# Moving loads to where their places come free in a one-core hybrid decoder step

## The chip, the cores and the metric

One core of a Trainium2 chip runs the whole program. TensorE (PE) does the matmuls, VectorE (DVE) and ScalarE (ACT) empty its PSUM banks and do the elementwise work, GpSimd (POOL) does little but issue stores, SyncE (SP) issues nearly all loads. The metric is the time of one execution in microseconds (us) on the device; lower is better. A profiled execution also has a span, from its first to its last instruction.

## The reference

One layer over 1024 prompt tokens and 8 sample tokens, all float32, width 1024. One input projection feeds three branches; each is gated, projected, and the sum goes through an output projection.

```python
h = rmsnorm(x, norm_gain)
proj = h @ w_in                                   # (T, 1024) x (1024, 10256)
q, k, v, gla_g, a_lr, u, pool_g, xq, xg, merge = split(proj)
o, S = gla_chunked(q, k, v, log_sigmoid(a_lr @ w_a2 + b_a) / 16, S0)   # 4 heads, 128 x 256 states
br_gla  = rmsnorm(o) * silu(gla_g)
br_pool = multiscale_pool(u, hist) * silu(pool_g)          # windows 2, 4, 8, 16
br_x    = cross_attn(xq, mem_k, mem_v) * silu(xg)          # 4 heads, 256 memory rows
merged  = sum_n sigmoid(merge_n) * (br_n @ w_branch[n])
y = rmsnorm(x + merged @ w_out)
```

For the prompt, the memory keys and values come from `mem_prompt`; for each of the 8 samples they are read from caches, as are the linear-attention state and the pooling history. New states, histories and memories are outputs too.

## The kernel before

Every large product is done in a split form: each float32 operand becomes a high and a low part (`split`: ScalarE writes the high part, VectorE the rest), and `mm3` does three matmuls, high by high, high by low, low by high.

The input projection runs in 36 pairs of 256 columns (`Pair`). Each pair is a 2 x 2 block product done with seven block products (Strassen's form); one product is 24 matmuls of 258 columns, in two halves `c`. `seq` is the order of all 252 products, `prepare` splits the left operands AHEAD products before they are used. A pair's weights arrive in two raw tiles (`raw`, three buffers); the first holds a11 and a21, the second a12 and a22. The sums of operands use `ws` tiles, the split parts `w2` tiles, two per product.

The mixers (cross attention, then linear attention, then pooling) are generators of steps. They are written between the products: after each half product, `fill` runs a `Stream` until the costs it has been given reach a target that grows with the slot number. Stream A holds cross and linear attention, stream B pooling. `mem` makes memory keys and values before that.

The order of instructions on TensorE and SyncE is the order in which they are written. For the other engines a planner orders them by its own estimates. Each queue is worked off in order: an instruction that waits holds all behind it.

Places for tiles: `R` is a shared ring of NR tiles of 128 x 512 (loads, split parts, outputs of the mixers), `V` four tiles of that size (sample loads kc, qb, vc, s0, vb, and raw output weights), `E` thirty tiles of 128 x 1032, `W2` ten, `PZ` two PSUM banks for the mixers, `PX` six for the products. A load into a tile waits on SyncE until the place is free.

For the samples of a head, cross attention writes their queries to memory (`xq_scr`) and reads them back spread over all partitions (`qb`), beside the cached keys (`kc`); `vc` are cached values. Linear attention does the same with `v_scr`, `vb` and the states `s0`. Both read-backs are issued from GpSimd's queue, the others from SyncE's. A stored branch output goes to `mix_scr` (`mixsc`) and is read back when its gate is ready.

After the pairs, 24 units of 72 matmuls do the branch projections (`fetch` loads and splits weights, one unit ahead), and then nine blocks of tokens are multiplied by `w_out`, whose 16 pieces `w_out_unit` loads and splits: `hf` is the half of the columns, `k` the row block.

Of the kernel before, what the change touches and what calls it, by code (L numbers as in the profile page):

```python
# [35 lines left out]
NE = 30  # L36
NR = 11
WORK_A, WORK_B = 500.0, 100.0
WINDOWS = (2, 4, 8, 16)
# [8 lines left out]
def trunk_kernel(ctx: ExitStack, tc: tile.TileContext,  # L48
# [75 lines left out]
    def W2(name, dt=F32R):  # L124
        return wk.tile([P, 4, P], dt, tag="w2", name=name, bufs=10)

# [98 lines left out]
    def split_r(src, shape, name, scale=None):  # L225
        hi, lo = R(shape, F32R, name + "h"), R(shape, F32R, name + "l")
        split(hi, lo, src, scale)
        return hi, lo

    def mm3(out, lh, ll, rh, rl, start, stop, more=False):  # L230

        nc.tensor.matmul(out, lhsT=lh, rhs=rh, start=start, stop=False, skip_group_check=more)  # L232
        nc.tensor.matmul(out, lhsT=lh, rhs=rl, start=False, stop=False, skip_group_check=more)  # L233
        nc.tensor.matmul(out, lhsT=ll, rhs=rh, start=False, stop=stop, skip_group_check=more)  # L234
# [37 lines left out]
    class Pair:  # L272


        def __init__(self, src, dst, s0=None, gated=None):
            self.src, self.dst, self.s0, self.gated = src, dst, s0, gated

        def load(self):
            self.raw = []
            for i in range(2):  # L280
                raw = RAW("raw")
                nc.sync.dma_start(out=raw, in_=self.src.rearrange("(k p) n -> p k n", p=P)[:, 4 * i:4 * i + 4])
                self.raw.append(raw)

        def operands(self):
            lo, hi = self.raw
            a11, a12, a21, a22 = lo[:, :, :P], hi[:, :, :P], lo[:, :, P:], hi[:, :, P:]

            def of(x, y, op):
                s = wk.tile([P, 4, P], F32, tag="ws", name="ws", bufs=3)  # L290
                nc.vector.tensor_tensor(s, x, y, op=op)
# [12 lines left out]
            yield parts(s1, "s1")  # L304
            yield parts(of(a11, a21, ALU.subtract), "s3")
            yield parts(of(a12, s2, ALU.subtract), "s4")
            yield parts(a22, "a22")
# [21 lines left out]
    RIGHT = ("11", "21", "t2", "t1", "t3", "22", "t4")  # L329
    AHEAD = 4  # L330
    left, prep = {}, {"n": 0}

    def prepare(n):

        while prep["n"] < min(n + 1, len(seq)):
            i, j = seq[prep["n"]]
            p = pairs[i]
            if j == 0:
                p.gen = p.operands()
            left[i, j] = next(p.gen)  # L340
            if j == 2 and i + 1 < NPAIR:
                pairs[i + 1].load()
            prep["n"] += 1

    pairs[0].load()
    for tb in range(4, 8):
# [235 lines left out]
    def cross_memory(h):  # L582
        mk, mv = cross["raw", h]
        t = PZ()
        for i in range(2):
            for a in range(2):
                nc.tensor.transpose(t[:, i * NM + a * P:i * NM + (a + 1) * P], mk[:, a, i * P:(i + 1) * P], ident)
        cross["mk", h] = split_r(t.rearrange("p (i m) -> p i m", i=2), [2, NM], "mkT")
        cross["mv", h] = split_r(mv, [2, DV], "mvs")
# [43 lines left out]

    def cross_sample(h):

# [7 lines left out]
        nc.gpsimd.dma_start(out=xq_scr[h], in_=qn[:NS])  # L643
        yield 1.2
        sc = wk.tile([P, 16], F32, tag="sc", name="sc", bufs=2)
        for b2 in range(4):
            qb = V([2, DV], name="qb")
            nc.gpsimd.dma_start(out=qb, in_=xq_scr[h][2 * b2:2 * b2 + 2].partition_broadcast(P))
            for bb in range(2):
                b = 2 * b2 + bb  # L650
                kc = loaded(ck[b, :, h, :].rearrange("(a p) d -> p a d", p=P), [2, DV], "kc", V)
                for a in range(2):
                    nc.vector.tensor_tensor_reduce(kc[:, a, :], kc[:, a, :], qb[:, bb, :],
                                                   scale=1.0, scalar=0.0, op0=ALU.mult, op1=ALU.add,
                                                   accum_out=sc[:, a * NS + b:a * NS + b + 1])
            yield 2.2
        yield 0.5
        yield 0.5
        yield 0.5
# [43 lines left out]
    def cross_steps():  # L703
# [14 lines left out]
        cross_load(0)  # L718
        cross_memory(0)
        yield 2  # L720
        cross_queries(0, 0)
        for s in range(16 + 2):
# [5 lines left out]
            if s % 4 == 3 and s < 15:  # L728
                cross_load(s // 4 + 1)
            if s >= 1:  # L730
                yield next(samples, 0)
            if 0 <= s - 2:
                values(s - 2)
                yield 1.7
            if s % 4 == 3 and s < 15:
# [125 lines left out]

    def gla_sample(h):

# [5 lines left out]
        nc.gpsimd.dma_start(out=v_scr[h], in_=vs[:NS])  # L869
        yield 1  # L870
        t = PZ()
# [8 lines left out]

        def states(b0):
            s0 = loaded(st_gla[b0:b0 + 2, h].rearrange("b k v -> k b v"), [2, DV], "s0", V)
            vb = V([2, DV], name="vb")
            nc.gpsimd.dma_start(out=vb, in_=v_scr[h][b0:b0 + 2].partition_broadcast(P))
            for i in range(2):
# [7 lines left out]
        sq = wk.tile([P, 2], F32, tag="sqs", name="sqs", bufs=2)  # L893
        for i in range(2):
            s0 = []
# [9 lines left out]
            nc.scalar.activation(t[:, :DV], t[:, :DV], AF.Square, accum_out=sq[:, i:i + 1])  # L905
            yield 1
        r = rstd_of(sq, 1.0 / DV)
        for i in range(2):
# [12 lines left out]
    def gla_steps():  # L921
# [7 lines left out]
        for n in range(N + 1):  # L929
# [8 lines left out]
            if n > 0:  # L938
                gla_recur(ph, 2 * pc + 1)
                yield 2  # L940
            if n < N:
                gla_within(h, 2 * c + 1)
                yield 2
                if n + 2 < N:
# [8 lines left out]
            if n >= 2:  # L953
                for _ in range(2):
                    yield next(samples, 0)
# [4 lines left out]

    def pool_steps():
        for g, w in enumerate(WINDOWS):
            raw = loaded(pool_w[g].rearrange("(k p) n -> p k n", p=P), [2, DV], "pwr")
            pw = split_r(raw, [2, DV], "pw")
            hist = R([DV], name="hist")
            nc.sync.dma_start(out=hist[:NS * HIST], in_=st_pool.rearrange("b j c -> (b j) c")[:, g * DV:(g + 1) * DV])
            us = smp_of(S_U + 2 * g, 2)
# [98 lines left out]
    class Stream:  # L1066


        def __init__(self, steps, work, first, last):
            self.steps, self.work, self.first, self.last, self.done = steps, work, first, last, 0  # L1070

        def run(self, slot):
            while self.done < self.work * (slot - self.first) / (self.last - self.first):
                cost = next(self.steps, None)
                if cost is None:
                    break
                self.done += cost
# [8 lines left out]
    def fill():  # L1086

        s = state["slot"] = state["slot"] + 1
        if s % 2 == 0:
            next(mem, None)  # L1090
        for stream in streams:
            stream.run(s)

    def emit(n, ahead=AHEAD):
# [6 lines left out]
        for _ in run_product(n):  # L1101
            fill()

# [211 lines left out]
```

## Time and profile before

| | |
|---|---|
| median of three runs | 1553.91 us |
| lowest, highest | 1551.36, 1558.27 us |
| profiled execution, its own time | 1558.15 us |
| its span | 1556.2 us |
| mean granted TensorE clock | 0.980 |
| DMA queues: SP, POOL (share of 16 engines) | 35.4%, 14.6% |

Busy time is a union: overlapping matmuls count once. In rows of instructions the columns are start, duration, engine, line, operation, what is written and read, shapes, and in brackets the idle time of the engine before it and what ended that. In rows of waits: who waited for whom, total us, number, longest. In rows of stretches: the stretch, its length, then busy time and number of instructions of the engines named, in the order PE, PE's weight loads, DVE, ACT, POOL (or PE alone), the granted clock, the share of the DMA engines, GB/s. In rows of DMAs: out and in, queue, number, size, median us from issue to landing. L232 to L234 are the three matmuls of `mm3`; L219 and L220 are `split`.

### The profile page before, as it was taken

The page shows a single profiled execution, that of the slowest core. Times are in us where ns is not written, and L with a number is a line of the kernel's source. Part 1 is how long each engine was busy: PE and PEld are TensorE (multiplying, and loading weights), DVE is VectorE, ACT ScalarE, POOL GpSimd, SP SyncE. Part 2 cuts the span into 40 slices and gives each one's busy share as a digit, 9 for nine tenths or more (in the row PEclk, how much of TensorE's full clock was granted, in tenths as well). Part 3 has the DMA queues.
Part 4 walks back from the last instruction along what each step waited for, and adds up shares of the span by engine and source line. Part 5 has one row for each costly group of instructions (what it writes and reads, how often), then busy time and mean ns, then how long its engine had stood idle before and what let it go on. Part 6 is the DMA issues. An engine that isn't in the chain of part 4 may idle for free.

```text
span 1556.2 us, 28209 instructions
## 1 busy us (share of the span) xinstructions
PE 1472.7 (95%) x10841; PEld 1399.4 (90%) x10841; DVE 882.6 (57%) x2043; ACT 682.6 (44%) x1564; POOL 174.8 (11%) x326
## 2 busy tenths in 40 slices
PE   4999999898999999999988999999999999999997
PEld 3898889898889999999977999999999999999785
DVE  4823646564566766667645586787544444544433
ACT  5523334343346656666654454444445332323311
POOL 1121101010101110111021111111000000011000
PEclk9999999999999999999999999999999999999999
DMA  6554546455544544454455445555648667542422
GB/s 221 157 189 136 171 133 214 156 182 156 183 152 129 174 141 134 141 158 144 128 156 158 155 150 182 185 168 178 203 151 262 229 231 253 181 131 87 146 86 70
DMA packets 180635, 255.25 MB, mean 164 GB/s; under 512 B 21397, under 2 KB 135725, under 8 KB 180493
## 3 DMA queue, kind: packets, MB, share of 16 engines
q1 hardware_dynamic: 155340, 169.56, 35.4%
q0 software_dynamic: 23936, 81.77, 14.6%
q8 instruction: 85, 1.39, 0.4%
q10 hardware_dynamic: 1224, 2.13, 0.4%
q14 instruction: 50, 0.40, 0.1%
HBM read 176.27 MB, written 77.59 MB: 163 GB/s over the span
## 4 chain that ended last, share of the span: by engine, by line
PE 64%; DMA 6%; issue 6%; DVE 3%; ACT 2%; POOL 1%; SPq 0%; DVEq 0%; POOLq 0%; ACTq 0%
PE px L232 19%; PE px L233 19%; PE px L234 19%; PE pz L232 1%; PE pz L233 1%; PE pz L234 1%; DMA vb<-vs 1%; DMA kc<-in_cache_mem_k_dram 1%; DMA mixsc<-xo 1%; DMA vc<-in_cache_mem_v_dram 1%; DMA wor<-in_w_out_dram 1%; PE pz L688 1%; DMA xq<-xqsc 1%; PE pz L810 1%; DMA qb<-xqs 1%
## 5 line engine op out<-in xcount | busy, mean ns | idle before, releaser
L232 PE MATMUL px<-bh,wbh 128*128 128x384 f32 (+1 forms) x576 | 185.3, 322 | 3.6 <-ACT bh L219 3.6
L234 PE MATMUL px<-bh,wbl 128*128 128x384 f32 (+1 forms) x576 | 185.1, 321 | 0.9 <-DVE wbl L220 0.9
L233 PE MATMUL px<-bl,wbh 128*128 128x384 f32 (+1 forms) x576 | 185.4, 322 | 0.2 <-DVE bl L220 0.2
L468 ACT ACTIVATE r<-px 128x258 f32<-128x258 f32 x240 | 90.4, 377 | 52.1 <-PE px L234 51.5
L232 PEld LDWEIGHTS px<-bh,wbh 128*128 128x128 f32 x576 | 109.2, 190 | 3.8 <-ACT bh L219 3.8
L234 PEld LDWEIGHTS px<-bh,wbl 128*128 128x128 f32 x576 | 109.1, 189 | 1.2 <-DVE wbl L220 1.2
L233 PEld LDWEIGHTS px<-bl,wbh 128*128 128x128 f32 x576 | 109.0, 189 | 0.6 <-DVE bl L220 0.6
L232 PE MATMUL px<-ot,s2h 128*128 128x258 f32 x320 | 96.4, 301 | 0.0
L232 PE MATMUL px<-o,a11h 128*128 128x258 f32 x320 | 94.6, 296 | 1.9 <-ACT a11h L219 1.9
L232 PE MATMUL px<-ot,a22h 128*128 128x258 f32 x320 | 94.0, 294 | 0.0
L232 PE MATMUL px<-ot,s1h 128*128 128x258 f32 x320 | 93.6, 292 | 0.0
L232 PE MATMUL px<-ot,s3h 128*128 128x258 f32 x320 | 93.4, 292 | 0.0
L232 PE MATMUL px<-o,s4h 128*128 128x258 f32 x320 | 93.3, 292 | 0.0
L232 PE MATMUL px<-o,a12h 128*128 128x258 f32 x320 | 93.2, 291 | 0.0
L234 PE MATMUL px<-ot,s2l 128*128 128x258 f32 x320 | 92.8, 290 | 0.0
L233 PE MATMUL px<-ot,s2h 128*128 128x258 f32 x320 | 92.5, 289 | 0.0
L234 PE MATMUL px<-o,a11l 128*128 128x258 f32 x320 | 91.0, 284 | 0.5 <-DVE a11l L220 0.5
L233 PE MATMUL px<-ot,a22h 128*128 128x258 f32 x320 | 91.4, 286 | 0.0
L234 PE MATMUL px<-ot,a22l 128*128 128x258 f32 x320 | 91.0, 284 | 0.0
L233 PE MATMUL px<-o,a11h 128*128 128x258 f32 x320 | 91.0, 284 | 0.0
L233 PE MATMUL px<-ot,s3h 128*128 128x258 f32 x320 | 90.9, 284 | 0.0
L233 PE MATMUL px<-ot,s1h 128*128 128x258 f32 x320 | 90.8, 284 | 0.0
(468 smaller groups left out, 4618.8 us busy)
## 6 DMA issues: line engine op xcount, KB each, us to landing
raw<-in_w_in_dram SPq DMA_DIRECT2D x80, 512.0 KB, 4.7
msc<-c POOLq DMA_DIRECT2D x24, 516.0 KB, 3.3
brsc<-c POOLq DMA_DIRECT2D x24, 516.0 KB, 4.0
sig<-msc SPq DMA_DIRECT2D x24, 516.0 KB, 6.9
mix<-mixsc SPq DMA_DIRECT2D x48, 256.0 KB, 3.7
wbr<-in_w_branch_dram SPq DMA_DIRECT2D x24, 512.0 KB, 5.5
brr<-brsc SPq DMA_DIRECT2D x48, 256.0 KB, 4.7
acc<-sig POOLq DMA_DIRECT2D x16, 516.0 KB, 3.7
```

The source lines that it names most:

```text
L232: nc.tensor.matmul(out, lhsT=lh, rhs=rh, start=start, stop=False, skip_group_check=more)
L233: nc.tensor.matmul(out, lhsT=lh, rhs=rl, start=False, stop=False, skip_group_check=more)
L234: nc.tensor.matmul(out, lhsT=ll, rhs=rh, start=False, stop=stop, skip_group_check=more)
L468: nc.scalar.activation(r, acc[c][:, :QT], AF.Copy)
L688: nc.tensor.matmul(t[32 * j:32 * j + 32, :DV], lhsT=pm[:, a, 4 * i + j, :], rhs=vc[j][:, a, :], start=a == 0, stop=a == 1)
L810: nc.tensor.matmul(t[0:64, 0:P], lhsT=ki[:, 0:64], rhs=qi, start=True, stop=True)
```

## The change

Loads of weights: each half is loaded after the last reader of the buffer that it takes. Mixers' loads (xq, kc, qb, s0, vb, pooling weights and history) are written one step before their use; qb and vb are issued from SyncE, and the queries and values of the next head are written to memory at the end of the head before. `fill` is called once per product, and stream B begins when A is over. The ring has 14 tiles, W2 has 8, ws 2, AHEAD is 3. `split_in` puts the low part into the raw tile. Linear attention takes sample steps at four places of its loop, and starts one chunk sooner. Output weights of the first half are kept in two V tiles (k = 0) and the ring; two units of the second half in W2.

```diff
-NR = 11
-WORK_A, WORK_B = 500.0, 100.0
+NR = 14
+WORK_A, WORK_B = 493.0, 108.0
...
-        return wk.tile([P, 4, P], dt, tag="w2", name=name, bufs=10)
+        return wk.tile([P, 4, P], dt, tag="w2", name=name, bufs=8)
...
+    def split_in(x, shape, name, scale=None):
+        hi, lo = R(shape, F32R, name + "h"), x.bitcast(F32R)
+        split(hi, lo, x, scale)
+        return hi, lo
...
-    AHEAD = 4
+    AHEAD = 3
...
-            if j == 2 and i + 1 < NPAIR:
-                pairs[i + 1].load()
+            if (i, j) == (0, 1):
+                pairs[1].load(0)
+            if j == 4 and i + 1 < NPAIR:
+                pairs[i + 1].load(1)
+            elif j == 6 and i + 2 < NPAIR:
+                pairs[i + 2].load(0)
...
+    def cross_fetch(h, c):
+        cross["xq", h, c] = loaded(chunk_of(xq_raw[h], c), [2, CT], "xq")
+
     def cross_queries(h, c):
-        raw = loaded(chunk_of(xq_raw[h], c), [2, CT], "xq")
-        cross["q", h, c] = split_r(raw, [2, CT], "xqs", 1.0 / 16.0)
+        cross["q", h, c] = split_in(cross["xq", h, c], [2, CT], "xqs", 1.0 / 16.0)
...
+        def fetch(b2):
+            kc = [loaded(ck[2 * b2 + bb, :, h, :]..., [2, DV], "kc", V) for bb in range(2)]
+            qb = V([2, DV], name="qb")
+            nc.sync.dma_start(out=qb, in_=xq_scr[h][2 * b2:2 * b2 + 2].partition_broadcast(P))
+            return kc, qb
+
+        kcs, qb = fetch(0)
...
-            yield 2.2
+            if b2 < 3:
+                kcs, qb = fetch(b2 + 1)
+                yield 1.2
+            elif h + 1 < NH:
+                cross_rows(h + 1)
+            yield 1
...
                 if s + 1 < 16:
-                    cross_queries((s + 1) // 4, (s + 1) % 4)
+                    cross_queries(*divmod(s + 1, 4))
+                if s + 2 < 16:
+                    cross_fetch(*divmod(s + 2, 4))
...
         for i in range(2):
+            fetched = [fetch(4 * i + b0) for b0 in (0, 2)]
+            yield 1
+            yield 0.5
             s0 = []
             for b0 in (0, 2):
-                s0.append(states(4 * i + b0))
-                yield 2
+                s0.append(states(4 * i + b0, *fetched[b0 // 2]))
+                yield 1.5
...
+        fetched = group_fetch(0)
         for g, w in enumerate(WINDOWS):
-            raw = loaded(pool_w[g]..., [2, DV], "pwr")
+            raw, hist = fetched
             pw = split_r(raw, [2, DV], "pw")
+            fetched = group_fetch(g + 1) if g < 3 else None
...
-        s = state["slot"] = state["slot"] + 1
-        if s % 2 == 0:
-            next(mem, None)
-        for stream in streams:
-            stream.run(s)
+        s = state["slot"] = state["slot"] + 2
+        next(mem, None)
+        streams[0].run(s)
+        if streams[0].over:
+            streams[1].run(s)
...
         for _ in run_product(n):
-            fill()
+            pass
+        fill()
...
-        if hf:
+        if hf and k < 2:
+            hi, lo = (W2("wo").rearrange("p a b -> p (a b)") for _ in range(2))
+        elif hf:
             e = E([2, 512], F32R, name="woe")
             hi, lo = e[:, 0], e[:, 1]
-        elif k < 3:
-            hi, lo = (W2("wo").rearrange("p a b -> p (a b)") for _ in range(2))
+        elif k < 1:
+            hi, lo = V([512], F32R, "woh"), V([512], F32R, "wol")
         else:
             hi, lo = R([512], F32R, "woh"), R([512], F32R, "wol")
```

More of the change, by code (lines that the diff above doesn't have):

```diff
@@ L275, in __init__, with load @@
         def __init__(self, src, dst, s0=None, gated=None):
[L276 to L283, printed above, removed]
+            self.src, self.dst, self.s0, self.gated, self.raw = src, dst, s0, gated, [None, None]
+        def load(self, i):
+            raw = RAW("raw")
+            nc.sync.dma_start(out=raw, in_=self.src.rearrange("(k p) n -> p k n", p=P)[:, 4 * i:4 * i + 4])
+            self.raw[i] = raw
         def operands(self):
@@ L287, in operands, with of @@
             a11, a12, a21, a22 = lo[:, :, :P], hi[:, :, :P], lo[:, :, P:], hi[:, :, P:]
-            def of(x, y, op):
-                s = wk.tile([P, 4, P], F32, tag="ws", name="ws", bufs=3)
+            def of(x, y, op, s=None):
+                s = wk.tile([P, 4, P], F32, tag="ws", name="ws", bufs=2) if s is None else s
                 nc.vector.tensor_tensor(s, x, y, op=op)
@@ L305, in operands @@
             yield parts(of(a11, a21, ALU.subtract), "s3")
-            yield parts(of(a12, s2, ALU.subtract), "s4")
+            yield parts(of(a12, s2, ALU.subtract, s2), "s4")
             yield parts(a22, "a22")
@@ L340, in prepare @@
             left[i, j] = next(p.gen)
-            if j == 2 and i + 1 < NPAIR:
-                pairs[i + 1].load()
+            if (i, j) == (0, 1):
[4 more added lines that the diff above has]
+                pairs[i + 2].load(0)
             prep["n"] += 1
-    pairs[0].load()
+    for i in range(2):
+        pairs[0].load(i)
     for tb in range(4, 8):
@@ L588, in cross_memory @@
         cross["mk", h] = split_r(t.rearrange("p (i m) -> p i m", i=2), [2, NM], "mkT")
-        cross["mv", h] = split_r(mv, [2, DV], "mvs")
+        cross["mv", h] = split_in(mv, [2, DV], "mvs")
+    def cross_fetch(h, c):
+        cross["xq", h, c] = loaded(chunk_of(xq_raw[h], c), [2, CT], "xq")
     def cross_queries(h, c):
-        raw = loaded(chunk_of(xq_raw[h], c), [2, CT], "xq")
-        cross["q", h, c] = split_r(raw, [2, CT], "xqs", 1.0 / 16.0)
+        cross["q", h, c] = split_in(cross["xq", h, c], [2, CT], "xqs", 1.0 / 16.0)
     def cross_scores(h, c):
@@ L632, in cross_values, with cross_rows @@
         nc.gpsimd.dma_start(out=mix_chunk(2, h, c), in_=g)
-    def cross_sample(h):
+    def cross_rows(h):
         xs = tiny(16, "xs").rearrange("p (i b) -> p i b", i=2)
@@ L643, in cross_sample @@
         nc.gpsimd.dma_start(out=xq_scr[h], in_=qn[:NS])
-        yield 1.2
-        sc = wk.tile([P, 16], F32, tag="sc", name="sc", bufs=2)
+    def cross_sample(h):
+        if h == 0:
+            cross_rows(0)
+            yield 1.2
+            yield 0.5
+            yield 0.5
+        sc = wk.tile([P, 16], F32, tag="sc", name="sc", bufs=2)
+        def fetch(b2):
+            kc = [loaded(ck[2 * b2 + bb, :, h, :].rearrange("(a p) d -> p a d", p=P), [2, DV], "kc", V) for bb in range(2)]
+            qb = V([2, DV], name="qb")
+            nc.sync.dma_start(out=qb, in_=xq_scr[h][2 * b2:2 * b2 + 2].partition_broadcast(P))
+            return kc, qb
+        kcs, qb = fetch(0)
+        yield 0.5
+        yield 0.5
         for b2 in range(4):
-            qb = V([2, DV], name="qb")
-            nc.gpsimd.dma_start(out=qb, in_=xq_scr[h][2 * b2:2 * b2 + 2].partition_broadcast(P))
             for bb in range(2):
-                b = 2 * b2 + bb
-                kc = loaded(ck[b, :, h, :].rearrange("(a p) d -> p a d", p=P), [2, DV], "kc", V)
+                b, kc = 2 * b2 + bb, kcs[bb]
                 for a in range(2):
@@ L655, in cross_sample @@
                                                    accum_out=sc[:, a * NS + b:a * NS + b + 1])
-            yield 2.2
-        yield 0.5
-        yield 0.5
+            if b2 < 3:
+                kcs, qb = fetch(b2 + 1)
+                yield 1.2
+            elif h + 1 < NH:
+                cross_rows(h + 1)
+            yield 1
         yield 0.5
@@ L719, in cross_steps @@
         cross_memory(0)
+        cross_fetch(0, 0)
         yield 2
         cross_queries(0, 0)
+        cross_fetch(0, 1)
         for s in range(16 + 2):
@@ L726, in cross_steps @@
                 if s + 1 < 16:
-                    cross_queries((s + 1) // 4, (s + 1) % 4)
-            if s % 4 == 3 and s < 15:
+                    cross_queries(*divmod(s + 1, 4))
+                if s + 2 < 16:
+                    cross_fetch(*divmod(s + 2, 4))
+            if s % 4 == 2 and s < 14:
                 cross_load(s // 4 + 1)
@@ L734, in cross_steps @@
                 yield 1.7
+            if s >= 1:
+                yield next(samples, 0)
             if s % 4 == 3 and s < 15:
@@ L860, in gla_out, with gla_rows @@
         nc.gpsimd.dma_start(out=mix_chunk(0, h, c), in_=g)
-    def gla_sample(h):
+    def gla_rows(h):
         t = PZ()
@@ L869, in gla_sample @@
         nc.gpsimd.dma_start(out=v_scr[h], in_=vs[:NS])
-        yield 1
+    def gla_sample(h):
+        if h == 0:
+            gla_rows(0)
+            yield 1
         t = PZ()
@@ L879, in gla_sample, with fetch, states @@
         ks = smp_of(S_K + h)[:, 0]
-        def states(b0):
+        def fetch(b0):
             s0 = loaded(st_gla[b0:b0 + 2, h].rearrange("b k v -> k b v"), [2, DV], "s0", V)
             vb = V([2, DV], name="vb")
-            nc.gpsimd.dma_start(out=vb, in_=v_scr[h][b0:b0 + 2].partition_broadcast(P))
+            nc.sync.dma_start(out=vb, in_=v_scr[h][b0:b0 + 2].partition_broadcast(P))
+            return s0, vb
+        def states(b0, s0, vb):
             for i in range(2):
@@ L894, in gla_sample @@
         for i in range(2):
+            fetched = [fetch(4 * i + b0) for b0 in (0, 2)]
+            yield 1
+            yield 0.5
             s0 = []
             for b0 in (0, 2):
-                s0.append(states(4 * i + b0))
-                yield 2
+                s0.append(states(4 * i + b0, *fetched[b0 // 2]))
+                yield 1.5
             yield 0.5
@@ L906, in gla_sample @@
             yield 1
+        if h + 1 < NH:
+            gla_rows(h + 1)
         r = rstd_of(sq, 1.0 / DV)
@@ L940, in gla_steps @@
                 yield 2
+                yield next(samples, 0)
             if n < N:
@@ L943, in gla_steps @@
                 yield 2
+                yield next(samples, 0)
                 if n + 2 < N:
@@ L952, in gla_steps @@
                 yield 2
-            if n >= 2:
-                for _ in range(2):
+            for _ in range(2):
+                if n >= 1:
                     yield next(samples, 0)
@@ L961, in pool_steps, with group_fetch @@
     def pool_steps():
+        def group_fetch(g):
+            raw = loaded(pool_w[g].rearrange("(k p) n -> p k n", p=P), [2, DV], "pwr", V)
+            hist = V([DV], name="hist")
+            nc.sync.dma_start(out=hist[:NS * HIST], in_=st_pool.rearrange("b j c -> (b j) c")[:, g * DV:(g + 1) * DV])
+            return raw, hist
+        fetched = group_fetch(0)
         for g, w in enumerate(WINDOWS):
-            raw = loaded(pool_w[g].rearrange("(k p) n -> p k n", p=P), [2, DV], "pwr")
+            raw, hist = fetched
             pw = split_r(raw, [2, DV], "pw")
-            hist = R([DV], name="hist")
-            nc.sync.dma_start(out=hist[:NS * HIST], in_=st_pool.rearrange("b j c -> (b j) c")[:, g * DV:(g + 1) * DV])
+            fetched = group_fetch(g + 1) if g < 3 else None
             us = smp_of(S_U + 2 * g, 2)
@@ L1069, in __init__ @@
         def __init__(self, steps, work, first, last):
-            self.steps, self.work, self.first, self.last, self.done = steps, work, first, last, 0
+            self.steps, self.work, self.first, self.last, self.done, self.over = steps, work, first, last, 0, False
         def run(self, slot):
@@ L1075, in run @@
                 if cost is None:
+                    self.over = True
                     break
```

## The prediction

> **What bounds the kernel now.** I read the page first, then TensorE's busy time by stretches, then the gaps of TensorE in the timeline, and last what the other engines and the two issuing queues waited for.
>
> ```profile
> span 1556.2 us, 28209 instructions
> PE 1472.7 (95%) x10841; PEld 1399.4 (90%) x10841; DVE 882.6 (57%) x2043; ACT 682.6 (44%) x1564; POOL 174.8 (11%) x326
> ```
>
> TensorE is the bound: 1556.2 - 1472.7 = 83.5 us of idle time is all that better timing can remove, and what a lower clock makes of the busy time. The stretches in which the mixers run (us, busy us and count of each engine, clock):
>
> ```profile
> 100.00:450.00 350.00, 321.36 (x2503) 304.41 (x2502) 181.70 (x458) 130.38 (x315) 46.82 (x90) 0.96 0.53 169
> 450.00:780.00 330.00, 326.51 (x2653) 311.62 (x2652) 224.55 (x588) 202.68 (x545) 41.48 (x70) 0.99 0.45 142
> 780.00:850.00 70.00, 57.36 (x425) 50.95 (x424) 33.17 (x87) 33.26 (x90) 17.05 (x29) 0.93 0.55 167
> ```
>
> Idle there: 28.6 us beside cross attention, 3.5 beside linear attention, 12.6 at its end; 44.8 in all. These are the eight gaps of 2 us and more (idle time and releaser in brackets):
>
> ```profile
> 183.91 0.38 PE L232 MATMUL pz<-mkTh,xqsh 128*128 128x256 f32 x1 [2.18 <-ACT xo L631]
> 205.17 0.58 PE L232 MATMUL pz<-mkTh,xqsh 128*128 128x256 f32 x1 [3.34 <-DVE pTl L220]
> 284.95 0.27 PE L674 MATMUL pz<-ident,ps 8*128 8x8 f32 x1 [3.90 <-ACT xo L631]
> 355.95 0.55 PE L232 MATMUL pz<-mkTh,xqsh 128*128 128x256 f32 x1 [3.35 <-DVE pTl L220]
> 432.86 0.38 PE L688 MATMUL pz<-vc,pm 128*32 128x256 f32 x1 [2.46 <-DMA vc<-in_cache_mem_v_dram]
> 579.96 0.32 PE L810 MATMUL pz<-kiqi 128*64 128x128 f32 x1 [2.09 <-DVE akvl L220]
> 792.10 0.44 PE L857 MATMUL pz<-ident,on 128*128 128x128 f32 x1 [4.53 <-ACT on L846]
> 835.12 0.64 PE L902 MATMUL pz<-s,pm 128*32 128x256 f32 x1 [5.17 <-DVE s L888]
> ```
>
> They sum to 27.0 us; 17.8 us lie in smaller gaps. The granted clock fell to half in nine stretches here, eight of them at these gaps. Their sum, the three that I shall not count as removed, and the two at the end of the linear attention:
>
> ```profile
> 147.05:150.47 3.42, 3.42 (x17) 0.50 0.38 155
> 433.77:437.19 3.42, 3.42 (x15) 0.50 0.77 235
> 580.55:583.96 3.41, 3.41 (x18) 0.50 0.45 119
> 792.17:795.58 3.41, 3.41 (x16) 0.50 0.73 209
> 833.13:839.96 6.83, 4.33 (x16) 0.50 0.34 117
> sum 40.95, PE 36.33; mean PE 4.04
> ```
>
> 36.33 us of matmuls at half speed cost half of it, 18.2 us. So at most 44.8 + 18.2 = 63 us can be won beside the mixers.
>
> Behind the gaps stand late loads. VectorE and ScalarE take their queues in order, so a wait for a load delays the eviction that TensorE needs:
>
> ```profile
> DVE kc L653 <- DMA kc<-in_cache_mem_k_dram: 19.3, 14, 5.7
> DVE s L888 <- DMA vb<-vs: 17.3, 5, 4.8
> DVE kc L653 <- DMA qb<-xqs: 7.8, 4, 3.0
> ACT xqsh L222 <- DMA xq<-xqsc: 18.3, 7, 7.8
> ACT pTh L219 <- DMA mixsc<-xo: 6.1, 2, 3.4
> ```
>
> The last row is no load: a new tile waits until the store of `xo` gives its place in the shared ring back. The chain of waits shows each cause at a gap (start, us):
>
> ```profile
> 277.65 5.18 DMA xq<-xqsc
> 350.20 4.79 DMA mixsc<-xo
> 827.56 5.73 DMA pwr<-in_pool_w_dram
> ```
>
> **The change, part by part.** *Loads of weights.* `load` issues both halves two steps before the second has a place, and SP stands still at it:
>
> ```profile
> SPq L766 <- PE pz L814: 83.1, 5, 20.0
> SPq L282 <- DVE ws L291: 75.0, 12, 12.9
> POOL mixsc L860 <- ACT go L859: 109.5, 14, 14.5
> ```
>
> The new places follow the last reader of each buffer, so most of these 75 us on L282 go. Behind them on SP stand all loads of the mixers; that is how xq and kc come late. The second half is then used four products after its issue. Prices:
>
> ```profile
> raw<-in_w_in_dram SPq DMA_DIRECT2D x80, 512.0 KB, 4.7
> kc<-in_cache_mem_k_dram SPq DMA_DIRECT2D x32, 256.0 KB, 4.4
> qb<-xqs POOLq DMA_DIRECT2D x16, 256.0 KB, 4.2
> ```
>
> ```profile
> 1100.00:1150.00 50.00, 50.00 (x419) 50.00 (x418) 30.76 (x59) 21.94 (x45) 3.28 (x5) 1.00 0.54 179
> 1200.00:1250.00 50.00, 50.00 (x319) 50.00 (x318) 18.61 (x36) 14.16 (x26) 2.13 (x4) 1.00 0.57 191
> ```
>
> A matmul of a product takes 50/419 = 0.119 us, a product of 24 takes 2.9 us, four take 11.5 us against 4.7 us to landing: hidden. If SP is held longer than 6 us there, a11 or a12 comes late and TensorE stops.
>
> *xq, kc, qb, s0, vb, pool weights one step ahead; qb and vb from POOL's queue to SP's.* 32 issues leave a queue whose single waits reach 14.5 us and join SP's. SP's share is 32 issues, about 0.4 us each as its other issues, 13 us on an engine that computes nothing. New waits on SP: `fetch` waits for a V place, hence for VectorE's use of the step before (kc) or for TensorE and the store of s0; behind it wait the loads of kq, v and raw, due one to four products later. Of the eight gaps I count six as removed (all but 432.86, whose vc loads are not moved, and 579.96, where VectorE was simply busy): 2.18 + 3.34 + 3.90 + 3.35 + 4.53 + 5.17 = 22.5 us. Of the 17.8 us of small gaps I take 12, an estimate: two thirds, as the chains at them lead to the same loads; the ends are 0 and 17.8. Clock: 18.2 less half of the three stretches above (5.1) leaves 13.1 us.
>
> The Trainium skill, "DMA: Bandwidth & Descriptors", section "Issuing engines are not separate DMA queues", says that the issuing engine changes only the time to initiate a DMA. The trace agrees on the transfer, 4.2 us from POOL beside 4.4 from SP for 256 KB. By that rule alone the move of queue is worth its issue time, which is the third rival below.
>
> *Ring of 14, `split_in` in place.* Each xq and each mv needs one tile less, and three more exist; against that one or two xq tiles are held early. The writer of the low half already waited for the high half: nothing added. This removes 205.17 and 355.95 above.
>
> *Once per product.* `fill` runs 2 x 493/329 = 3.0 units of steps after 24 matmuls in place of half that after 12. Laying the steps against the targets I count 47 fills with two or more TensorE steps, 4 before. Three places become worse: the first memory step and the first scores share a fill (half a product less cover, 1.4 us); kc is used for two pairs in one fill once (1 to 2 us of VectorE); the second four vc tiles of heads 0 and 3 get their places one product before use, 2.9 us and one step of cover for four loads (about 1 us). With one more half-clock stretch (1.7 us) I give back 6 us; ends 0 and 20.
>
> The linear-attention samples start one chunk earlier and get four steps per chunk, not two; by my count none is left behind the main steps, where 792.10 and 835.12 stand now.
>
> *AHEAD 3, W2 of 8, two ws.* A split (0.63 + 0.69 us, rows below) has three products, 8.6 us, in place of four. In the branch stage the second half of the next weights waits for the unit before; 72 matmuls x 50/319 = 11.3 us cover it. Zero, within 1 us each; if ScalarE came to be 8 us late, TensorE would stop.
>
> *The output weights.* This part costs. `w_out_unit(0, 0)` keeps two of the four V places to the end, so the raw tiles of the other loads rotate through two.
>
> ```profile
> 1434.96 0.33 SPq L1185 DMA_DIRECT2D acc<-acc  x1
> 1435.34 17.31 SPq L567 DMA_DIRECT2D wor<-in_w_out_dram  x12
> ...
> L219 ACT ACTIVATE woh<-wor x4: 632/632/635, 1439.7 to 1443.4; 128x512 fp32r<-128x512 f32 x4
> L220 DVE TENSOR_TENSOR wol<-wor,woh x4: 691/692/693, 1440.4 to 1444.1; 128x512 fp32r<-128x512 f32 x4
> DMA to landing us min/median/max: 2.9/3.0/3.0
> ```
>
> Twelve loads cannot start before 1434.96, when SP passes the load of acc. With four places they went in three rounds; with two they need six, each 3.0 + 0.63 + 0.69 + 0.33 = 4.7 us: 28 us, and some 2.5 us while VectorE evicts the last unit. The last weight is split near 1435.3 + 28 + 2.5 = 1466, against about 1458 now: 8 us, in three gaps of 2 to 3 us. Those can halve the clock for the bursts between; I add 2. The ends are 3 (rounds as short as they can be, W2 places early for two units) and 14 (rounds of 6 us). I take 10.
>
> The Trainium skill, "TensorE: Matmul & The Clock Gate", section "Why this matters for your kernels", warns only of idle gaps over about 3 us. The trace differs: the gap of 2.09 us at 579.96 was followed by half clock at 580.55. By the rule in the Trainium skill the output stage would cost 8 and the time be 1520; I give that 0.2 of the forecast's chance and go by the trace.
>
> Sum: 22.5 + 12 + 13.1 - 6 - 10 = 31.6 us. The profiled execution took 1558.15 us, so 1526.6; it lies 4.2 above the median of the runs shown, 1553.91, hence 1522.3.
>
> **Rivals.** *The output stage costs nothing more* (SP gets ahead of the acc load, or the splits are quicker): 1522 - 10 = 1512. Against it, SP's waits at L1185 are for a tile of another pool that the change leaves alone.
>
> *SP stays blocked.* The waits of L766 (longest 20 us) are on ring tiles read late by TensorE; if they persist, one step ahead is not enough, and only the end of the linear attention is won: 4.53 + 5.17 us and half of 3.41 + 4.33, some 13.6, less 16 for give-back and output. About 1556, no change.
>
> *The change of queue does nothing*: vb and qb remain late, the gaps at 792.10 and 835.12 stay with their clock, 13.6 us less gain: 1536. Against it, each is also moved a step earlier. This is what the rule cited from the Trainium skill's "DMA: Bandwidth & Descriptors" would give.
>
> *Slower: two steps in one fill.* The mixers have two pz banks. If the second step of each of the 47 double fills waits for its operands or bank, the point of no gain is 31.6/47 = 0.67 us a fill; at 1 us the time is 1522 + 47 = 1569. Against it: bank reuse still has 24 matmuls between, as two halves of 12 had, and the one clean case of a late eviction now is 2.09 us at 579.96.
>
> **How the numbers follow.** The runs shown spread over 0.45%, so 0.5% (7.8 us) is about what can be told from no change. Forecast 0.53, no output cost 0.17, queue does nothing 0.10, SP blocked 0.11, slower 0.09. The first three are faster: 0.80; same 0.11; slower 0.09. Of the forecast alone the range is 1512 to 1537, half of its terms' spans to each side (6 + 6 + 7 below, 12 + 14 + 4 above). Low end: all small gaps gone (6), nothing given back (6), output at 3 (7), 1503, put at 1500; the high end reaches into the blocked case, 1550.
>
> **What would show it.** Right: the waits of xqsh on xq, kc on kc and qb, s on vb fall to a few us; L282 hardly waits; fewer than four half-clock stretches between 100 and 850; the last twelve wor loads spread over 26 us or more, with gaps of TensorE behind woe. Wrong: many gaps of about 1 us on pz released by VectorE or ScalarE, L766 or the fetches of kc holding SP for 10 us and more, or TensorE waiting for a11 and a12.

## The result, and the profile after

| | median of the runs (lowest to highest) | profiled execution | span | clock |
|---|---|---|---|---|
| before | 1552.63 us (1550.06 to 1558.27) | 1558.15 us | 1556.2 us | 0.980 |
| after | 1511.42 us (1509.88 to 1513.71) | 1512.94 us | 1511.2 us | 0.988 |

The ratio is 0.9731, with a 95% interval of 0.9699 to 0.9763: 41 us faster. The forecast was 1522 in a range of 1500 to 1550. The old kernel has one more run here than in the table above. Its profiled execution was 5.5 us slower than its median and the changed kernel's 1.5 us, so 4 of the 45 us between the two profiles lie in the executions.

The page's first lines, and the stretches beside cross attention, beside linear attention and at its end (columns as before; the last line is the output stage):

```profile
span 1511.2 us, 28154 instructions
PE 1456.6 (96%) x10841; PEld 1386.9 (92%) x10841; DVE 880.5 (58%) x2043; ACT 678.9 (45%) x1564; POOL 158.0 (10%) x294
```

```profile
100.00:450.00 350.00, 338.75 (x2744) 324.09 (x2743) 201.54 (x516) 149.91 (x369) 42.77 (x82) 0.99 0.56 179
450.00:740.00 290.00, 290.00 (x2386) 277.18 (x2385) 202.94 (x530) 181.79 (x497) 37.16 (x61) 1.00 0.48 156
740.00:800.00 60.00, 57.03 (x462) 54.09 (x461) 33.27 (x85) 31.56 (x86) 8.02 (x14) 0.97 0.44 146
1384.00:1410.00 26.00, 22.50 (x98) 16.47 (x97) 13.55 (x20) 8.97 (x13) 4.13 (x6) 0.91 0.47 147
```

VectorE and ScalarE are busy within 4 us of what they were. What went is 28.9 us of TensorE's idle time (83.5 to 54.6) and 16.1 us of its busy time, about 9 of that through the clock. Idle beside the mixers is 11.3 + 0 + 3.0 = 14.2 us, where it was 44.8: 30.6 us less. TensorE at half speed, here by stretches of TensorE alone:

```profile
145.94:149.35 3.41, 3.19 (x14) 0.50 0.96 251
316.61:320.02 3.41, 2.96 (x14) 0.50 0.01 2
784.24:787.65 3.41, 3.41 (x18) 0.50 0.08 28
sum 10.23, PE 9.56; mean PE 3.19
```

Three stretches in place of nine, 4.8 us of loss in place of 18.2: 13.4 us less between these two executions. The old kernel was timed 44 more times beside the experiments below, at a clock of 0.981 to 0.988 with a median of 0.985; its profiled execution had 0.980, so a usual run had less of this to win. What VectorE and ScalarE waited for, against the rows of before (the waits of `xqsh` on xq, of `kc` on its own load and of `pTh` on the store of xo are gone):

```profile
DVE kc L679 <- DMA qb<-xqs: 24.7, 12, 4.4
DVE s L931 <- DMA vb<-vs: 14.2, 9, 3.0
DVE ws L295 <- DMA raw<-in_w_in_dram: 11.6, 12, 3.2
```

The two largest rows of TensorE's waits between 100 and 850, of ten that are left there:

```profile
PE pz L652 <- DVE mkTl L220: 3.2, 1, 3.2
PE pz L892 <- ACT on L881: 2.9, 1, 2.9
```

And what SP waited for at the loads of weights, now L286:

```profile
SPq L286 <- DVE a22l L220: 100.3, 12, 18.1
SPq L286 <- DVE ws L295: 99.5, 13, 11.7
SPq L286 <- DVE rv L247: 46.3, 4, 12.5
```

The last view is a surprise: SP stands longer at these loads than before (the row with ws was 75.0), not shorter. Its waits for ring tiles (L766 before, 83.1 us in one row) are gone.

One pair of rows splits the gain by stage. The load of acc in the output stage started at 1434.96 before; now:

```profile
1382.59 0.33 SPq L1243 DMA_DIRECT2D acc<-acc  x1
1382.97 24.85 SPq L577 DMA_DIRECT2D wor<-in_w_out_dram  x12
```

The splits of these raw tiles, and the time from issue to landing, from the view of the tile `wor`:

```profile
L219 ACT ACTIVATE woe<-wor x6: 629/629/631, 1400.1 to 1410.3; 128x512 fp32r<-128x512 f32 x6
DMA to landing us min/median/max: 2.5/2.7/2.9
```

So 52.4 us were won up to here, 30.6 + 13.4 = 44.0 of them seen as idle time and clock beside the mixers. The span is 45.0 us shorter, so 7.4 us were lost behind it. The remaining 8.4 us of the gain lie in startup (0.7) and in busy time at full clock: with half of what ran at half clock taken off, TensorE's busy time over the whole span is 1448.2 us before and 1441.0 after, for the same 10841 matmuls. No view attributes these 7 us, and the ends of matmuls are modelled, so their cause stays open.

### The profile page after: what moved, and what is told of

Its sections match the earlier page's. It is cut to its first block, busy times and chain, and to the rows that moved or that the text cites. A ratio compares the mean times of both kernels' runs of the same rounds, so it can differ in the third digit from the quotient of the medians.

```text
span 1511.2 us, 28154 instructions
## 1 busy us (share of the span) xinstructions
PE 1456.6 (96%) x10841; PEld 1386.9 (92%) x10841; DVE 880.5 (58%) x2043; ACT 678.9 (45%) x1564; POOL 158.0 (10%) x294
## 4 chain that ended last, share of the span: by engine, by line
PE 89%; DMA 6%; DVE 3%; ACT 1%; issue 1%; SPq 0%; DVEq 0%; ACTq 0%
PE px L238 25%; PE px L239 24%; PE px L240 24%; PE pz L393 4%; DMA qb<-xqs 2%; PE pz L238 2%; PE pz L240 2%; PE pz L239 2%; DMA raw<-in_w_in_dram 2%; DMA wor<-in_w_out_dram 1%; PE pz L863 1%; PE pz L845 1%; PE px L424 1%; DMA vc<-in_cache_mem_v_dram 1%; PE pz L847 1%
## 5 line engine op out<-in xcount | busy, mean ns | idle before, releaser
L238 PE MATMUL px<-ot,s2h 128*128 128x258 f32 x320 | 93.8, 293 | 0.0
L238 PE MATMUL px<-o,s4h 128*128 128x258 f32 x320 | 93.3, 291 | 0.3 <-DVE c L543 0.3
L238 PE MATMUL px<-ot,s3h 128*128 128x258 f32 x320 | 92.8, 290 | 0.0
L239 PE MATMUL px<-ot,s2h 128*128 128x258 f32 x320 | 91.3, 285 | 0.0
L240 PE MATMUL px<-ot,s1l 128*128 128x258 f32 x320 | 90.8, 284 | 0.0
L239 PE MATMUL px<-o,s4h 128*128 128x258 f32 x320 | 90.6, 283 | 0.0
```

## The experiments

The theories were: the loads written one step ahead carry the gain; the places of the weights' loads do; the pace of the linear-attention samples does; GpSimd's queue was the trouble. Against the rhythm of once per product stood a theory that it costs something. Undoing a part of the changed kernel, or adding it to the old one, tells them apart. Lines "-" of a diff are the changed kernel's. Each ratio is to the old kernel timed beside that run; its medians there were 1552.0 to 1553.7 us. The changed kernel itself was not timed again beside its variants, so a difference of a few us between two of them is not safe: the intervals of `no_ahead`, `no_split_in` and `wo_raw` overlap with its own, 0.9699 to 0.9763, and that of `half_fill` touches it.

| run | median us (lowest to highest) | ratio to before, 95% |
|---|---|---|
| half_fill | 1503.92 (1499.66 to 1506.17) | 0.9684, 0.9656 to 0.9712 |
| no_ahead | 1515.19 (1513.47 to 1516.61) | 0.9759, 0.9735 to 0.9784 |
| raw_old | 1550.69 (1547.82 to 1552.87) | 0.9987, 0.9973 to 1.0002 |
| raw1_old | 1554.57 (1552.84 to 1555.77) | 1.0022, 1.0008 to 1.0036 |
| qb_vb_pool | 1526.27 (1523.55 to 1526.41) | 0.9828, 0.9807 to 0.9849 |
| gla_pace | 1532.12 (1525.20 to 1533.65) | 0.9866, 0.9840 to 0.9893 |
| no_split_in | 1515.68 (1514.15 to 1517.45) | 0.9770, 0.9749 to 0.9790 |
| wo_raw | 1506.64 (1505.74 to 1510.64) | 0.9710, 0.9683 to 0.9736 |
| before_raw | 1545.69 (1542.47 to 1549.83) | 0.9958, 0.9939 to 0.9976 |
| before_fill | 1549.30 (1544.77 to 1555.90) | 0.9982, 0.9964 to 1.0000 |
| before_three | 1526.99 (1524.43 to 1528.48) | 0.9840, 0.9819 to 0.9862 |
| best | 1496.51 (1494.61 to 1502.14) | 0.9655, 0.9632 to 0.9679 |

### Where the weights' loads are written

`raw_old` writes both halves at the old place; `raw1_old` leaves the first half at its new place and moves only the second back.

```diff
 # raw_old
-            if (i, j) == (0, 1):
-                pairs[1].load(0)
-            if j == 4 and i + 1 < NPAIR:
+            if j == 2 and i + 1 < NPAIR:
+                pairs[i + 1].load(0)
                 pairs[i + 1].load(1)
-            elif j == 6 and i + 2 < NPAIR:
-                pairs[i + 2].load(0)
 # raw1_old
-            if j == 4 and i + 1 < NPAIR:
+            if j == 2 and i + 1 < NPAIR:
```

> The changed kernel with both halves of the next pair's weights issued together two steps before the second has a place, as before; all else as changed. Theory D (SP standing still at these loads made the mixers' loads late): 20 us or more slower, 1531 and up, with SP waits at the raw load against the ws tile of 75 us or more and late xq and kc. Theory A (one step ahead is enough to hide SP's standing still): 0 to 10 us slower, 1511 to 1521.

> The changed kernel with the load of the second half alone written two steps earlier (where a12's place is not yet free), the first half where the change has it. Theory D: this is the load that waits for the ws tile, so all the loss of raw_old returns, 1540 to 1552. Rival (the loss came from the first half being fetched late): within 5 us of 1511.

Both lose the whole gain: 39 and 43 us. So the place of one load of 512 KB for each pair, two products earlier or later, decides all of it while every other part of the change stays in. SP's queue shows how. The timeline of SP in `raw_old` (start, duration, line, out and in, count):

```profile
233.40 13.93 SPq L286 DMA_DIRECT2D raw<-in_w_in_dram  x2
247.44 1.47 SPq L574 DMA_DIRECT2D xq<-xqsc  x1
...
250.08 0.94 SPq L574 DMA_DIRECT2D kc<-in_cache_mem_k_dram  x2
251.07 0.78 SPq L666 DMA_DIRECT2D qb<-xqs  x1
251.90 8.20 SPq L574 DMA_DIRECT2D kc<-in_cache_mem_k_dram  x2
260.42 0.34 SPq L666 DMA_DIRECT2D qb<-xqs  x1
```

The same stretch in the changed kernel:

```profile
234.51 0.37 SPq L286 DMA_DIRECT2D raw<-in_w_in_dram  x1
234.93 3.40 SPq L577 DMA_DIRECT2D kc<-in_cache_mem_k_dram  x2
238.65 0.34 SPq L669 DMA_DIRECT2D qb<-xqs  x1
242.43 0.52 SPq L577 DMA_DIRECT2D xq<-xqsc  x1
243.01 1.74 SPq L577 DMA_DIRECT2D kc<-in_cache_mem_k_dram  x2
246.27 0.34 SPq L669 DMA_DIRECT2D qb<-xqs  x1
249.08 0.37 SPq L286 DMA_DIRECT2D raw<-in_w_in_dram  x1
```

In `raw_old` the two halves hold SP for 13.93 us, and the pairs of kc come behind it one after another, the last with its qb at 265.83 (next fence); in the changed kernel two pairs with their qb are issued in that same time. The late pairs then queue on VectorE. The chain of waits in `raw_old` (start, duration, what):

```profile
265.83 4.28 DMA qb<-xqs
...
271.85 0.61 DVE mkTl L220
```

And the stall of TensorE that ends it, in the timeline:

```profile
272.51 0.38 PE L649 MATMUL pz<-ident,xs 128*8 128x128 f32 x1 [5.21 <-DVE mkTl L220]
```

`mkTl` has nothing to do with kc: it empties one of the mixers' two PSUM banks and stands behind kc on VectorE. TensorE waits 5.21 us for that bank. One chain holds the whole path, from SP's wait at the weights for VectorE to another stall of TensorE, of 3.40 us:

```profile
398.06 0.61 DVE ws L295
...
398.68 0.37 SPq L286
...
400.16 5.61 DMA qb<-xqs
...
407.18 0.37 PE pz L688
```

Between 100 and 850 `raw_old` has eight gaps of 2 us and more. What ended them leads back, in seven, to a load of the mixers (four times qb, and mkv, xq and s0 once each), in one to raw itself. Beside cross attention TensorE then idles this much:

```profile
100.00:450.00 350.00, 324.76 (x2561) 309.65 (x2560) 185.67 (x472) 135.81 (x328) 39.97 (x75) 0.96 0.54 171
```

25.2 us and a clock of 0.96, close to the figures of before (28.6, 0.96). The totals of the waits don't show this: all rows of SP's waits at L286 between 100 and 800 sum to 389 us in the changed kernel and 412 in `raw_old`, and VectorE's waits for qb are 24.7 and 24.9. So what counts is not how long SP waits, but what is due behind the wait.

`before_raw` puts these places alone into the old kernel.

> The kernel before with one edit: each half of the next pair's weights is loaded where its place comes free, as in the change; AHEAD 4, ring of 11, mixers' loads in the step of use, qb and vb from POOL, half-product rhythm, output weights as before. Theory D (the place of the weights' loads in SP's order is the cause of nearly the whole gain): 1508 to 1525; since the output stage and the rhythm of before are each better by 5 to 8 us, it could even pass the changed kernel. Theory E (the place of the loads is needed, but it pays only with the larger ring and the loads one step ahead): 1535 to 1550.

It wins 6 us. The places are needed and not enough: in the old kernel SP still stands at the ring (87.9 us in the row of `L769`, the old L766), and xq, kc and the store of xo are still late (waits of 14.6, 12.5 and 5.6 us, where they were 18.3, 19.3 and 6.1).

### The loads one step ahead

`no_ahead` moves all loads of the mixers (xq, kc and qb, s0 and vb, pooling) back into the step that uses them; two of its edits:

```diff
-        kcs, qb = fetch(0)
...
         for b2 in range(4):
+            kcs, qb = fetch(b2)
...
-                s0.append(states(4 * i + b0, *fetched[b0 // 2]))
+                s0.append(states(4 * i + b0, *fetch(4 * i + b0)))
```

> The changed kernel with every mixers' load (xq, kc and qb, s0 and vb, pooling weights and history) written back into the step that uses it; places of the weights' loads, ring and rhythm as changed, all issued from SP. Theory A (writing them one step ahead is what removes the stalls): 20 to 40 us slower than the changed kernel, 1531 to 1551, with xqsh waiting for xq and VectorE for kc again. Theory D (SP merely had to be free of the weights' loads; it runs ahead by itself): within 8 us of 1511.

It costs 3.8 us, and the two ranges touch, so it may be nothing. The waits of `xqsh` on xq come back, 9.1 us in 5 waits, at almost no price. The part that I had put first is nearly worthless by itself once nothing blocks SP.

### The queue of qb and vb

```diff
-            nc.sync.dma_start(out=qb, in_=xq_scr[h]...)
+            nc.gpsimd.dma_start(out=qb, in_=xq_scr[h]...)
 # and vb in the same way
```

> The changed kernel with qb and vb issued from POOL's queue again, one step ahead as changed. If the issuing queue does nothing: within 3 us of 1511. If POOL's waits of up to 15 us make them late: 1516 to 1530, with longer waits of VectorE for qb and vb than the 25 and 14 us of the changed kernel.

14.9 us are lost. GpSimd's queue in this kernel:

```profile
POOL mixsc L644 <- ACT xo L643: 62.2, 10, 14.8
POOL out_dram L932 <- DVE s L931: 60.0, 15, 11.2
POOL qb L669 <- DVE sc L679: 36.5, 7, 5.8
```

The stores on it wait for results, up to 14.8 us, with the read-backs in line behind them; the read-backs wait for their own places, with stores behind. VectorE's waits for qb rose from 24.7 to 31.8 us, those for vb fell from 14.2 to 11.1. So the price of the queue is measured, but which of these delays makes it is not shown. The Trainium skill, "DMA: Bandwidth & Descriptors", section "Issuing engines are not separate DMA queues", gives the choice of engine no more than the time to initiate. That agrees with the transfers themselves, 4.6 us from issue to landing for qb here and 4.5 in the changed kernel; it does not cover an issuing queue in which other instructions wait, and here the measurement decides.

### The pace of the linear-attention samples

```diff
-                yield next(samples, 0)        # two places of the loop over chunks
...
-            for _ in range(2):
-                if n >= 1:
+            if n >= 2:
+                for _ in range(2):
                     yield next(samples, 0)
```

> The changed kernel with the sample steps of linear attention given out as before: two per chunk, from the third chunk on, so that the last heads' steps are left to the end of stream A. Theory F (the crowd of sample steps at the end, where 12.6 us of idle time and 4 us of half clock stood, is a separate cause): 1521 to 1530, with the gaps again in the last 60 us before pooling. Rival (those gaps came from vb and SP alone): within 4 us of 1511.

20.7 us; the median lies just above the forecast of 1521 to 1530. The samples lag behind the main steps again, and the end of linear attention comes back. TensorE's waits from 740 to 820 in `gla_pace`:

```profile
PE pz L948 <- DVE s L931: 7.1, 2, 3.6
PE pz L963 <- ACT os L957: 5.2, 2, 3.2
```

And the stretch:

```profile
740.00:820.00 80.00, 66.35 (x487) 58.70 (x486) 35.17 (x92) 36.00 (x102) 12.07 (x21) 0.91 0.52 164
```

13.7 us idle, and a clock of 0.91, where the changed kernel has 3.0 us and 0.97 in its last 60 us. VectorE waits 18.5 us for vb there, and 2.4 in the changed kernel's last 60 us. That fits a reading in which a load's delay becomes TensorE's when no other work is left between one sample step and the next; it was not tested further.

### Low parts in place, and three parts on the old kernel

`no_split_in` gives each low part a ring tile of its own again.

```diff
-        hi, lo = R(shape, F32R, name + "h"), x.bitcast(F32R)
+        hi, lo = R(shape, F32R, name + "h"), R(shape, F32R, name + "l")
```

> The changed kernel with the low parts of xq and mv in ring tiles of their own again, so two to four of the fourteen tiles fewer are free. If ring places still hold the mixers up: 1516 to 1530, with waits for the store of xo back on ScalarE or VectorE. If fourteen tiles are ample: within 3 us of 1511.

4.3 us, between the two expectations; the waits for the store of xo did not come back, so nothing shows that it is ring places that cost these us. `before_three` adds to the old kernel the places of the weights' loads, qb and vb on SP, and the pace of the samples.

> The kernel before with three edits: places of the weights' loads, qb and vb issued from SP, sample steps of linear attention at four places per chunk from the second chunk on. Ring of 11, AHEAD 4, loads in the step of use, half-product rhythm, output weights as before. If these three causes add up: 1545.7 less 15 (queue) less some 12 (pace) = 1515 to 1524. If the ring of 11 still holds SP (its waits for ring places were 153 us on the loads of kq): 1528 to 1545.

It wins 25.5 us: 750 to 820 is as good as in the changed kernel, and the rest stays in cross attention, with SP held by the ring. SP's waits, and the stretches:

```profile
SPq L769 <- PE pz L817: 130.4, 9, 21.8
```

```profile
100.00:450.00 350.00, 327.46 (x2589) 311.11 (x2588) 188.50 (x474) 137.51 (x330) 40.95 (x77) 0.97 0.53 173
750.00:820.00 70.00, 69.31 (x567) 66.12 (x567) 45.65 (x123) 41.85 (x113) 7.23 (x13) 1.00 0.39 126
```

It lies a little above the forecast of parts that add up and just below the one in which the ring binds. The changed kernel is 16 us faster, although it has the slower rhythm and output stage of the next two sections. Which of the ring's size, the low parts in place and the loads ahead brings these us was not separated; the ring's size alone wasn't tried.

### The rhythm

`half_fill` calls `fill` after each half product again; `before_fill` puts the new rhythm into the old kernel.

```diff
 # half_fill
-        s = state["slot"] = state["slot"] + 2
-        next(mem, None)
+        s = state["slot"] = state["slot"] + 1
+        if s % 2 == 0:
+            next(mem, None)
...
         for _ in run_product(n):
-            pass
-        fill()
+            fill()
```

> The changed kernel with one edit: the mixers' steps are given out after each half product again (slot targets as before), loads as changed. Theory A (late loads were the stall; fewer alternations between a product's and the mixers' matmuls gave the 7 us by which TensorE's busy time fell beyond the clock): busy time of TensorE up by 5 to 8 us, idle time between 100 and 800 us near 14 us as in the changed kernel, time 1516 to 1521. Theory B (the rhythm removed the stalls, since each step has a whole product behind it): the eight gaps return, 1540 or more. Theory C (two steps in one fill cost): faster than 1511.

> The kernel before with one edit: mixers' steps given out once per product. From half_fill (7.5 us faster than the changed kernel) theory C says that the coarser rhythm costs: 1555 to 1563. Rival (a whole product between groups of steps gives late loads more time): 1540 to 1550.

`half_fill` is 7.5 us faster than the changed kernel, and their ranges lie apart. The theory that fewer alternations save busy time is refuted (1456.6 us before this edit, 1448.3 with it), and so is the one that the rhythm removed the stalls. Beside cross attention and at the end of linear attention:

```profile
100.00:450.00 350.00, 342.63 (x2819) 330.07 (x2818) 208.98 (x537) 156.69 (x383) 44.93 (x84) 1.00 0.57 183
740.00:800.00 60.00, 58.11 (x484) 55.66 (x483) 36.99 (x92) 31.40 (x84) 8.55 (x15) 1.00 0.52 169
```

Idle time falls by 3.9 + 1.1 us, and no stretch here is at half clock. This profile is of the fastest of the four executions, at a clock of 0.992; the others had 0.988 and 0.989, like the changed kernel, so how much of the 7.5 us is the clock stays open. In the old kernel the new rhythm cost nothing: `before_fill` is 2.7 us faster, inside the rival's 1540 to 1550, with an interval that reaches 1.0000. That it costs there is refuted; that it helps is not shown. Perhaps the rhythm doesn't decide while TensorE stalls on late loads anyway.

### The output weights

`wo_raw` loads the raw tiles of the second half into the three buffers of the input weights, which are free by then, and not into V.

```diff
-        raw = loaded(w_out[...], [512], "wor", V)
+        raw = (RAW("wor").rearrange("p a b -> p (a b)")[:, :512] if hf else V([512], name="wor"))
+        nc.sync.dma_start(out=raw, in_=w_out[...])
```

> The changed kernel with the raw tiles of the second half of the output weights taken from the three raw-weight buffers, which are free by then, not from the two V places that are left. Theory A (the output stage's 7.4 us are the two places): the twelve loads go out in some 17 us, not 25, the half-clock stretch at the first block of tokens goes, 1503 to 1506. Rival (VectorE's evictions and the split of the last merged tile are what the first block waits for): within 2 us of 1511.

4.8 us faster, just above the 1503 to 1506 of the forecast; the ranges overlap by 0.8 us, but the mechanism shows in the trace of `wo_raw`, in SP's timeline and in the stretch:

```profile
1384.94 19.12 SPq L1261 DMA_DIRECT2D wor<-in_w_out_dram  x12
```

```profile
1384.00:1410.00 26.00, 24.68 (x122) 20.09 (x121) 15.36 (x24) 10.68 (x15) 4.62 (x6) 1.00 0.57 183
```

The loads take 19.12 us in place of 24.85, and the clock stays whole. From the load of acc to the end of the span it is 121 us, as in the old kernel (129 in the changed one): the whole loss of this stage is won back.

### Both together

`best` is the changed kernel with `half_fill` and `wo_raw`.

> The changed kernel with the half-product rhythm (half_fill, 7.5 us faster) and the raw tiles of the second half of the output weights in the raw-weight buffers (wo_raw, 4.8 us faster). They lie in different stages, so they should add up: 1498 to 1501. If the rhythm's gain was partly in the output stage: 1502 to 1504.

1496.51 us beats both kernels, and its interval lies clear of that of the changed one: 3.4% faster than before, where the changed kernel is 2.7%. The two parts add up, to a little more than the 1498 to 1501 expected. TensorE's longest wait between 100 and 850 is now 2.2 us.

## Why the prediction was right or wrong

In the profiled executions 45.2 us went, where the sum had 31.6. The time fell on the number of the first rival, in which the output stage costs nothing (1512), and just below the forecast's own 1512 to 1537; but the output stage did cost 7.4 us. The number alone would have picked the wrong account.

*Where idle time and clock would go* was right in the main. Of the six gaps that were to go, five went; the one at `on` (792.10 before) shrank from 4.53 to 2.9 us, and half clock at 784.24 follows it still. The one at `akvl`, taken as VectorE being busy, went too, and a new one of 3.2 us came. The clock gave 13.4 us for 13.1, with three half-clock stretches, under the four named. That match is partly luck: of the three stretches that were to stay only the one at 147.05 did (now 145.94), those at 433.77 and 580.55 went, and the one behind `on`, which was to go, and a new one behind the gap of 3.2 us stand in their place. Net of the give-back, idle time and clock were put at 41.6 us and gave 44.0; the other 8.4 have almost no term in the sum.

*"Most of these 75 us on L282 go"* failed. They rose. The step took the length of a wait for its cost; `raw_old` shows that the cost lies in the loads due behind it. The conclusion, that the mixers' loads come in time, held for xq and kc all the same. The transfer of the second half was called hidden; it isn't quite: VectorE waits 11.6 us in 12 waits for it at `ws`, and the chain ahead of the gap at `on` leads through one of them, to a load of raw.

*What carries the gain* was not weighed rightly. I described the loads one step ahead as the remedy of most gaps; undone, they cost 3.8 us. The place of the second half of the weights costs 39 to 43, the pace of the samples 20.7, the queue 14.9, the low parts in place 4.3. These add up to more than the 41 us that were won: the parts aren't independent. Perhaps each stall makes VectorE and SP late for what follows.

*qb and vb*: the queue was worth its change, but the waits of `kc` on qb were to fall to a few us and rose from 7.8 to 24.7. With four V places qb is issued only when VectorE has done with the pair before, so VectorE waits for each transfer; the chain ahead of TensorE's new gap of 3.2 us, at the bank that `mkTl` empties, leads there. The rival that the queue does nothing is refuted by `qb_vb_pool`; so is SP stays blocked in the form I gave it, since the ring's waits went.

*Once per product*: 6 us were given back, `half_fill` measured 7.5. Size right; that it comes from the three places named was not tested, and the point of no gain, 0.67 us a fill, was far away: 7.5 us over the 47 double fills of the count are 0.16 us each.

*The output stage*: 10 forecast, 7.4 measured. The cause is the one named, two places for the raw tiles, as `wo_raw` shows. The twelve loads took 24.85 us against 28 forecast, in part since a round was shorter: 2.7 us to landing, not 3.0. The split of the price was wrong: 8 us of waiting in gaps of 2 to 3 us and 2 us for the clock were expected. The gaps were under 0.8 us, the clock still fell (below), and half of the 9.38 us busy at half clock, 4.7 us, is the larger part of the 7.4.

What the sum had too small is thus the gain up to the load of acc, 52.4 for 41.6 net. Most of that difference is the 7 us of busy time at full clock, for which the sum had no term and the runs show no cause.

## What to carry to other kernels

In an in-order queue of loads, ask of each wait what is due behind it. Write a load where its place has just come free, not where it is first possible: here one early load for each pair cost the whole gain, while nearly as many us of waits at the same line, with nothing due behind them, cost almost nothing. Parts of such a change hide one another, so undo each from the finished kernel as well as adding it to the old one: the same edit was worth 6 us one way and 39 the other. When the stalls are gone, look again at what seemed free before, as the rhythm of the steps and the buffers of the last stage were here.

## What the hardware showed

The granted clock halved in a stage without a gap of even 1 us. Behind the output weights, in the changed kernel, TensorE's timeline (two of its rows) and its stretches:

```profile
1402.88 0.49 PE L238 MATMUL px<-woe,mg3h 128*128 128x512 f32 x1 [0.64 <-ACT woe L219]
1405.10 0.50 PE L238 MATMUL px<-woe,mg4h 128*128 128x512 f32 x1 [0.76 <-ACT woe L219]
```

```profile
1400.40:1405.46 5.06, 2.96 (x8) 1.00 0.50 153
1405.46:1415.70 10.24, 9.38 (x20) 0.50 0.48 155
```

For 5.06 us TensorE was busy 2.96, in bursts of one or two matmuls with gaps of 0.2 to 0.8 us; then it had half the clock for 10.24 us, though it was busy for 9.38 of them. In `wo_raw`, where this stage is denser, the clock stayed whole. The Trainium skill, "TensorE: Matmul & The Clock Gate", section "Why this matters for your kernels", asks for no idle gap over about 3 us between bursts; that was met here and did not keep the clock. What share of busy time does keep it, these runs don't tell.
